# Stick-breaking attention with the scores laid out by key, and running sums made by matrix products

## The chip, the cores and the metric

The kernel runs on one core of one Trainium2 chip. The metric is device time in microseconds (us) of one execution; the times below are medians of repeated runs. The profile is one execution recorded by the hardware profiler.

## The reference

One transformer-like layer on a (2048, 1024) input: a normalised input is projected, three mixers work side by side (attention with 8 heads, a gated convolution, a spatial gate), their results are projected back, and an MLP of width 4096 follows. Only the attention is changed:

```python
z = jnp.einsum('bqhd,bkhd->bhqk', q_blk, k_ctx) * scale
mask = s_pos[None, :] < t_pos[:, None]
log_beta = jax.nn.log_sigmoid(z)
log_stay = jnp.where(mask, jax.nn.log_sigmoid(-z), 0.0)
log_after = lax.cumsum(log_stay, axis=3, reverse=True) - log_stay
w = jnp.where(mask, jnp.exp(log_beta + log_after), 0.0)
outs.append(jnp.einsum('bhqk,bkhd->bqhd', w, v_ctx))
```

With softplus(z) = log(1 + e^z), the weight is exp(z minus the sum of softplus over this key and all later allowed keys). So each query needs a running sum over keys, from the last key backwards.

## The kernel before

The sequence is cut into two halves of 1024 tokens and groups of 512 (`gl` = 0, 1). Every product with weights is made in three passes of 32-bit operands split into a high and a low part (`split`: a cast to the high part on ACT, a subtraction for the low part on DVE). A segment (`run(seg, ...)`) walks over blocks of units; a unit is 256 columns of a weight matrix. Segments 0 and 1 make the projections of the two halves; `take_u` and `take_v` are the spatial gate (tiles pu, pvs, then pmix), VUnit makes pv, QK makes pq and pk, Conv makes pc. Segments 2 and 3 make the output projection (tile po). Then `Up` and `Down` make the MLP (pa, pb, pc, py).

Attention runs behind this as generators. A task is one head and 256 queries (two blocks of 128); each block of queries looks at its own 128 keys and the 128 before. There are 64 tasks. `Background.tick()` is called after each product of a unit: it takes every active generator one `yield` further and starts one task from the queue. So the steps of a task stand one tick apart, with one large product (24 matmuls of 128x512, or 48 of 128x256) between ticks:

- at its first tick: scores z (queries on partitions, two sets of 256 keys as columns) with a mask added by a bf16 product, then `weights`: softplus on ACT and DVE (L434 to L437), a backward scan for each block of queries (L440), the total of each query saved in `carry` (L441), z minus the scan (L442), exp (L443);
- two ticks later: four transposes of the weights into the PSUM tile wt (L467) and their split into wT;
- one tick later: the product with the values (av, L479), and its two halves added (L483, L484).

`all_gone(half)` takes the minimum of `carry` over all tasks of a half. A far-key branch (`far_keys`) is taken only if that minimum is too small, which does not happen in the runs. On PE the minimum needs one transpose (tile pcm), which stands between the first block's group 0 and group 1 of segments 1 and 2. The order of instructions on each engine is fixed when the program is built, by a scheduler that follows the order of the code where it can. Each engine runs its list in order. DMAs are issued from SP (`load`) and from POOL (`store`).

## Time and profile before

| | |
|---|---|
| median of 3 runs | 2228.54 us (2227.8 to 2235.25) |
| the profiled execution | 2228.7 us, its span 2226.9 us |
| mean granted TensorE clock | 0.984 |
| busy: PE, DVE, ACT, POOL | 95%, 65%, 46%, 16% of the span |
| attention's first and last product on PE | at 142.9 and 757.6 us |

The span is the time from the first to the last instruction of the profiled execution; 1.8 us of its time lie outside. PE is the tensor engine, DVE the vector engine, ACT the scalar engine. A busy time is the union of the instructions' times. Matmuls overlap, so what one of them costs PE is the distance between starts in a timeline, and not its duration.

### The profile page before, as it was taken

The numbers are of one execution on the slowest core, as the hardware profiler recorded it, in microseconds if no ns is written. First come the engines' busy times: TensorE is split into PE (matmuls) and PEld (weight loads), VectorE is DVE, ScalarE is ACT, GpSimd is POOL, SyncE is SP. The second block draws the span as 40 slices with busy tenths as digits, with TensorE's granted clock in tenths as the row PEclk, the third lists the DMA queues.
The fourth block names the chain that finished last, engine by engine and source line by source line (L and its number), as shares of the span: only waits on it lengthen the run. The fifth ranks groups of instructions, "written<-read, shape, count | busy, mean of one in ns | idle before, by whom it ended". The sixth has DMA issues, their size and how long they took to land.

```text
span 2226.9 us, 30078 instructions
## 1 busy us (share of the span) xinstructions
PE 2119.3 (95%) x11039; PEld 1802.1 (81%) x11039; DVE 1456.2 (65%) x2417; ACT 1020.5 (46%) x1728; POOL 348.0 (16%) x589
## 2 busy tenths in 40 slices
PE   3999999999999989988999999999999999999998
PEld 3887888788788989876788878888788888888886
DVE  6788877677767643676767787677743434347675
ACT  4645656746556324265444454444523323224432
POOL 2020211021211112223322222222200000000010
PEclk9999999999999999999999999999999999999999
DMA  7473553343434466978956586565764435447572
GB/s 274 130 211 119 148 161 109 98 131 90 126 110 142 155 212 215 357 268 281 332 186 214 201 297 213 189 218 193 259 204 152 152 121 171 142 123 230 195 246 85
DMA packets 223215, 415.35 MB, mean 187 GB/s; under 512 B 18400, under 2 KB 106416, under 8 KB 223056
## 3 DMA queue, kind: packets, MB, share of 16 engines
q1 hardware_dynamic: 177424, 264.28, 37.1%
q0 software_dynamic: 45504, 149.00, 19.1%
q8 instruction: 89, 1.46, 0.3%
q14 instruction: 70, 0.57, 0.1%
q10 hardware_dynamic: 128, 0.04, 0.0%
HBM read 262.18 MB, written 142.67 MB: 182 GB/s over the span
## 4 chain that ended last, share of the span: by engine, by line
PE 51%; issue 11%; DMA 4%; DVE 3%; POOL 2%; ACT 1%; POOLq 0%; SPq 0%; DVEq 0%; ACTq 0%
PE py L1190 27%; PE pb L1082 9%; PE pc L1082 6%; PE pa L1082 5%; PE pc L269 1%; DMA hr<-hs 1%; POOL x L771 1%; DMA f<-in_mlp_w_dram 1%; PE pv L278 1%; PE pq L269 0%; DMA hs<-hs 0%; POOL hd L994 0%; DMA hr<-hd 0%; DVE h L130 0%; POOL hs L1008 0%
## 5 line engine op out<-in xcount | busy, mean ns | idle before, releaser
L1190 PE MATMUL py<-h,w 128*128 128x512 f32 x2688 | 610.7, 389 | 0.0
L1190 PEld LDWEIGHTS py<-h,w 128*128 128x128 f32 x2688 | 504.7, 188 | 105.5 <-issue 1.0
L130 DVE TENSOR_TENSOR w<-ar,w 128x1024 fp32r<-128x1024 f32 x112 | 137.0, 1223 | 264.1 <-ACT w L127 263.8
L127 ACT CAST w<-ar 128x1024 fp32r<-128x1024 f32 x112 | 118.0, 1053 | 368.9 <-PE py L1190 347.8
L127 ACT CAST w<-raw 128x512 fp32r<-128x512 f32 (+1 forms) x215 | 155.2, 736 | 127.9 <-PE pc L1082 46.6
L278 PE MATMUL po<-w,h 128*128 128x256 f32 x1536 | 194.3, 288 | 4.1 <-PEq L681 2.4
L1082 PE MATMUL pb<-h,w 128*128 128x512 f32 x768 | 188.9, 395 | 9.3 <-DVE s L1051 7.8
L130 DVE TENSOR_TENSOR w<-raw,w 128x512 fp32r<-128x512 f32 (+1 forms) x215 | 177.1, 835 | 29.5 <-ACT w L127 28.4
L1082 PE MATMUL pa<-h,w 128*128 128x512 f32 x768 | 189.5, 394 | 6.4 <-ACT s L1049 4.9
L1082 PE MATMUL pc<-hx,w 128*128 128x512 f32 x768 | 190.6, 396 | 4.6 <-DVE hid L1056 4.6
L278 PEld LDWEIGHTS po<-w,h 128*128 128x128 f32 x1536 | 190.2, 196 | 4.7 <-issue 4.2
L1082 PEld LDWEIGHTS pb<-h,w 128*128 128x128 f32 x768 | 145.7, 191 | 42.2 <-DVE s L1051 7.6
L1082 PEld LDWEIGHTS pa<-h,w 128*128 128x128 f32 x768 | 144.8, 189 | 39.2 <-ACT s L1049 5.7
L1082 PEld LDWEIGHTS pc<-hx,w 128*128 128x128 f32 x768 | 143.8, 188 | 39.6 <-DVE hid L1056 5.5
L269 PE MATMUL pc<-h,w 128*128 128x512 f32 x576 | 137.3, 394 | 0.0
L269 PEld LDWEIGHTS pc<-h,w 128*128 128x128 f32 x576 | 106.6, 188 | 21.2
L1057 ACT ACTIVATE hid<-hid 128x512 f32<-128x512 f32 x96 | 60.6, 631 | 106.0 <-DVE hid L1056 106.0
L1082 PE MATMUL pb<-hx,w 128*128 128x512 f32 x384 | 96.9, 402 | 4.5 <-DVE s L1051 4.5
L1289 POOL DMA_DIRECT2D out_dram<-y x24 | 13.0, 540 | 559.9 <-DVE y L1288 558.6
L278 PE MATMUL pv<-w,h 128*128 128x256 f32 x768 | 99.5, 285 | 0.0
L278 PEld LDWEIGHTS pv<-w,h 128*128 128x128 f32 x768 | 94.5, 191 | 0.1
L269 PE MATMUL pk<-h,w 128*128 128x512 f32 x384 | 94.4, 399 | 0.1
(217 smaller groups left out, 3319.7 us busy)
## 6 DMA issues: line engine op xcount, KB each, us to landing
ar<-ad SPq DMA_DIRECT2D x112, 512.0 KB, 4.0
ad<-hid POOLq DMA_DIRECT2D x128, 256.0 KB, 3.2
raw<-in_mlp_w_dram SPq DMA_DIRECT2D x62, 512.0 KB, 5.3
ad<-hsum POOLq DMA_DIRECT2D x96, 256.0 KB, 3.4
aw<-in_ada_w_dram SPq DMA_DIRECT2D x32, 512.0 KB, 4.7
f<-in_mlp_w_dram SPq DMA_DIRECT2D x32, 512.0 KB, 4.9
w2s<-f POOLq DMA_DIRECT2D x64, 256.0 KB, 3.4
w<-w2s SPq DMA_DIRECT2D x32, 512.0 KB, 3.7
```

What stands on the lines that cost most here:

```text
L127: A.copy(hi, src)
L130: V.tensor_tensor(lo, src, hi.bitcast(F32), ALU.subtract)
L269: T.matmul(ps, lhsT=w[k][:, a, c0:c0 + P], rhs=hT[k][:, b], start=n == 0, stop=n == 3 * KT - 1)
L278: T.matmul(ps, lhsT=hT[k][:, a, tb * P:(tb + 1) * P], rhs=w[k][:, b], start=n == 0, stop=n == 3 * KT - 1)
L771: store(out=x1d[g][t0:t0 + 2 * P, cl].rearrange("(b p) n -> p b n", p=P), in_=t.rearrange("p (b n) -> p b n", b=2))
L1057: A.activation(t, t, AF.Relu)
L1082: T.matmul(ps[key], lhsT=w[:, a, k * P:(k + 1) * P], rhs=h[k // 2][:, b, k % 2], start=start and m == 0, stop=m == 11, skip_group_check=no ...
L1190: T.matmul(ps[tb], lhsT=self.a[q][:, a, u * G + tb * P:u * G + (tb + 1) * P], rhs=self.w[at, c][:, b, u], start=c == 0 and u == 0 and n == ...
L1289: (load if end else store)(out=out2[t0:t0 + P, sl], in_=y)
```

## The change

Scores are made with keys on partitions: the keys are the stationary operand and the queries the moving one, so z holds for each block of queries its columns for the 128 keys before (z4[:, b, 0]) and for its own 128 keys (z4[:, b, 1]). The mask is added by one product with F32R operands. Softplus is split into two tiles and multiplied by a triangular matrix of -1 (`neg_after`), which adds the negative running sum within a block of keys onto z in PSUM, and by a matrix of -1 (`neg_ones`), which adds the total of the own block to the block before. The exponential of z is then already laid out for the product with the values, and the transposes are gone. The totals of the queries lie in one row: a copy of row 0 of z from before the sums, minus row 0 after; this row is stored to memory (`cs`) for each task, and `all_gone` loads it back.

z now lives from the first tick to two ticks later, so its pool has three buffers in place of two; the bank of wt is given up. `ones` becomes `neg_ones` (with a subtraction where it was an addition), sums of `mod_sum` are kept in the loaded tile, and some small tiles move to the pool of `etile`.

```diff
-        pz = ph.enter_context(tc.tile_pool(name="pz", bufs=2, space=PSUM, reuse_waits="tile"))
+        pz = ph.enter_context(tc.tile_pool(name="pz", bufs=3, space=PSUM, reuse_waits="tile"))
...
-            A.activation(e, z, AF.Abs)
-            A.activation(e, e, AF.Exp, scale=-1.0)
-            A.activation(e, e, AF.Ln, bias=1.0)
-            V.scalar_tensor_tensor(e, z, 0.0, e, ALU.max, ALU.add)
-            for a, b in lo:
-                r = e[:, a:b][:, ::-1]
-                V.tensor_tensor_scan(r, r, r, init, ALU.add, ALU.bypass)
-            V.tensor_copy(save, e.rearrange("p (b k) -> p b k", b=len(lo))[:, :, 0])
+        def softplus(e, z):
+            A.activation(e, z, AF.Abs)
+            A.activation(e, e, AF.Exp, scale=-1.0)
+            A.activation(e, e, AF.Ln, bias=1.0)
+            V.scalar_tensor_tensor(e, z, 0.0, e, ALU.max, ALU.add)
...
             z = pz.tile([P, G], F32, name="z", tag="z")
-            last = None
-            for b in range(2):
-                o = (2 * qp + b) * P
-                c0 = 256 * b if first and b == 0 else 256 * b + P
-                zb = z[:, b * 256:(b + 1) * 256]
-                with tc.issue_after(last.ins) if last is not None else nullcontext():
-                    T.matmul(zb, lhsT=qq[:, 0, o:o + P], rhs=kk[:, o:o + 256], start=True, stop=False)
-                    T.matmul(zb, lhsT=qq[:, 1, o:o + P], rhs=kk[:, o:o + 256], start=False, stop=False)
-                    last = T.matmul(z[:, c0:(b + 1) * 256], lhsT=identb, rhs=mask[:, c0 - 256 * b:256],
-                                    start=False, stop=True)
+            z4 = z.rearrange("p (b w t) -> p b w t", b=2, w=2)
+            n = 0
+            for kb, c0, w, o in ((1, P, 256, 0), (0, 0, P, 0), (2, 384, P, P)):
+                for s in range(2):
+                    T.matmul(z[:, c0:c0 + w], lhsT=kk[:, q0 + kb * P:q0 + (kb + 1) * P],
+                             rhs=qq[:, s, q0 + o:q0 + o + w], start=n == 0, stop=False)
+                    n += 1
+            T.matmul(z4[:, :, 1], lhsT=identr, rhs=mask.unsqueeze(1).to_broadcast([P, 2, P]),
+                     start=False, stop=True)
             e = etile()
-            weights(e, z, ((0, 256), (256, G)), 0.0, carry[:, half, h, ib:ib + 2])
+            softplus(e, z)
+            sT = halves("sT")
+            split(sT[:, 0], sT[:, 1], e, A)
+            row = etile("row")[0:1]
+            A.copy(row[:, 0:256].rearrange("p (b t) -> p b t", b=2), z4[0:1, :, 0])
             yield
             yield
-            wt = pw.tile([P, G], F32, name="wt", tag="wt")
-            for m in range(4):
-                T.transpose(wt[:, m * P:(m + 1) * P], e[:, m * P:(m + 1) * P], ident)
-            wT = pl.tile([P, 2, G], F32R, name="wT", tag="wT")
-            split(wT[:, 0], wT[:, 1], wt, A)
+            s4 = sT.rearrange("p s (b w t) -> p s b w t", b=2, w=2)
+            for s in range(2):
+                T.matmul(z, lhsT=neg_after, rhs=sT[:, s], start=False, stop=False,
+                         skip_group_check=True)
+            for s in range(2):
+                T.matmul(z4[:, :, 0], lhsT=neg_ones, rhs=s4[:, s, :, 1], start=False, stop=s == 1,
+                         skip_group_check=True)
+            e = etile()
+            A.activation(e, z, AF.Exp)
+            V.tensor_tensor(row[:, 256:].rearrange("p (b t) -> p b t", b=2),
+                            row[:, 0:256].rearrange("p (b t) -> p b t", b=2), z4[0:1, :, 0],
+                            ALU.subtract)
+            store(out=cs[half][h:h + 1, ib * P:(ib + 2) * P], in_=row[:, 256:])
+            wT = halves("wT")
+            split(wT[:, 0], wT[:, 1], e, A)
...
-            store(out=cs[half].rearrange("h p i -> p h i"), in_=carry[:, half])
+            first = (1 - half) * 2 * P
+            n = (HALF - first) // 16
+            ca = etile("ca")[:, :n]
+            load(out=ca, in_=cs[half][:, first:].rearrange("h (a n) -> h a n", n=n))
             cm = sp.tile([P, 1], F32, name="cm", tag="cm")
-            V.tensor_reduce(cm, carry[:, half, :, 2 - 2 * half:], AX.XY, ALU.min)
+            V.tensor_reduce(cm, ca, AX.X, ALU.min)
```

The first place is one tick of segment 0 on PE, after the product pq of group 0 (h_... are the buffers of the input tile). Before:

```order
L269 MATMUL pq<-h_300,w 128x512 x6
L479 MATMUL av<-wT,vt 128x256 x2
L479 MATMUL av<-wT,vt 128x128 x4
L467 MATMUL wt<-ident,e 128x128 x4
L457 MATMUL z<-kk,qq 128x256
L458 MATMUL z<-kk,qq 128x256
L459 LDWEIGHTS identb
L459 MATMUL z<-mask,identb 128x128
L457 MATMUL z<-kk,qq 128x256
L458 MATMUL z<-kk,qq 128x256
L459 LDWEIGHTS identb
L459 MATMUL z<-mask,identb 128x128
```

The same tick in the changed kernel:

```order
L275 MATMUL pq<-h_302,w 128x512 x6
L506 MATMUL av<-wT,vt 128x256 x2
L506 MATMUL av<-wT,vt 128x128 x4
L484 MATMUL z<-sT,neg_after 128x512 x2
L487 MATMUL z<-sT,neg_ones 128x2x128 x2
L469 MATMUL z<-qq,kk 128x256 x2
L469 MATMUL z<-qq,kk 128x128 x4
L472 MATMUL z<-mask,identr 128x2x128
L275 MATMUL pk<-h_299,w 128x512 x6
```

The four transposes of an older task give way to four products of its softplus, and the scores of the new task are six products and one with the mask.

The second place (place A) is on PE in segment 1, from the last product pvs of group 0 to the first product pu of group 1. Before:

```order
L278 MATMUL pvs<-w,h_3627 128x256 x6
L670 MATMUL pcm<-ident,cm 1x128 [waits DVE_49]
L269 MATMUL pu<-h_4014,w 128x512 [waits PE_49,Activation_49]
L269 MATMUL pu<-h_4014,w 128x512 x5
L269 MATMUL pu<-h_4015,w 128x512 x6
L269 MATMUL pu<-h_4016,w 128x512 x6
L652 MATMUL pmix<-swT,vn 128x256 [waits DVE_49]
L652 MATMUL pmix<-swT,vn 128x256 x3
```

In the changed kernel (rows of products pmix left out in the middle):

```order
L284 MATMUL pvs<-w,h_3733 128x256 x5
L679 MATMUL pmix<-swT,vh 128x256 [waits DVE_49]
...
L679 MATMUL pmix<-swT,vh 128x256 [waits PE_49]
L679 MATMUL pmix<-swT,vl 128x256 [waits DVE_49]
...
L679 MATMUL pmix<-swT,vl 128x256
L700 MATMUL pcm<-identr,cm 1x128 [waits DVE_49]
L275 MATMUL pu<-h_4136,w 128x512 [waits Activation_49]
L275 MATMUL pu<-h_4136,w 128x512 x5
```

21 products pmix, 12 of the first pair of token blocks and 9 of the second, now stand ahead of pcm and pu, where 18 products pu stood ahead of the first pmix.

The third place (place B) is on PE in segment 2, around the transposed minimum pcm. Before:

```order
L278 MATMUL po<-w,h_7293 128x256 x6
L479 MATMUL av<-wT,vt 128x256 [waits DVE_49,Activation_49]
L479 MATMUL av<-wT,vt 128x256 [waits DVE_49]
L479 MATMUL av<-wT,vt 128x128 x4
L467 MATMUL wt<-ident,e 128x128 [waits PE_49]
L467 MATMUL wt<-ident,e 128x128 x3
L670 MATMUL pcm<-ident,cm 1x128
L278 MATMUL po<-w,h_7628 128x256 x6
```

In the changed kernel:

```order
L506 MATMUL av<-wT,vt 128x128 x4
L484 MATMUL z<-sT,neg_after 128x512 x2
L487 MATMUL z<-sT,neg_ones 128x2x128 x2
L506 MATMUL av<-wT,vt 128x256 [waits DVE_49,Activation_49]
L506 MATMUL av<-wT,vt 128x256 [waits DVE_49]
L506 MATMUL av<-wT,vt 128x128 x4
L700 MATMUL pcm<-identr,cm 1x128 [waits DVE_49]
L284 MATMUL po<-w,h_7879 128x256 x6
```

The running sums of the last task, its product av and the minimum over all stored rows now follow each other with no product po between them; before, the last av stood 48 products po later and pcm waited for nothing new.

## Rows read from the trace of the kernel before

**Rows 1.** The page: span and busy time of the engines.
```profile
span 2226.9 us, 30078 instructions
PE 2119.3 (95%) x11039; PEld 1802.1 (81%) x11039; DVE 1456.2 (65%) x2417; ACT 1020.5 (46%) x1728; POOL 348.0 (16%) x589
```

**Rows 2.** Windows: busy us of each engine (x count), granted clock, DMA share, GB/s.
```profile
140.00:760.00 620.00, 599.57 (x3648) 525.24 (x3647) 459.85 (x869) 356.18 (x644) 94.28 (x155) 0.98 0.43 131
219.00:225.00 6.00, 6.00 (x25) 5.33 (x25) 4.63 (x10) 3.44 (x7) 1.16 (x2) 0.50 0.13 30
360.00:420.00 60.00, 54.48 (x315) 46.26 (x313) 48.43 (x92) 49.70 (x91) 4.64 (x9) 0.94 0.35 108
```

**Rows 3.** Attention's PE groups: count, busy us, mean ns, idle before, what ended it.
```profile
L479 PE MATMUL av<-wT,vt 128*128 128x128 f32 (+1 forms) x368 | 53.4, 274 | 6.1 <-DVE wT L130 3.1 <-ACT wT L127 2.0 <-DVE a_sb L484 0.9
L457 PE MATMUL z<-kk,qq 128*128 128x256 f32 x128 | 46.6, 365 | 5.4 <-DVE kk L527 3.4 <-DVE carry L441 1.2 <-DVE e L442 0.8
L467 PE MATMUL wt<-ident,e 128*128 128x128 f32 x256 | 41.3, 283 | 4.0 <-DVE wT L130 3.7 <-DVE kk L520 0.3
```

**Rows 4.** PE's timeline around two ticks: start us, duration, line, count.
```profile
304.27 0.79 PE L479 MATMUL av<-wT,vt 128*128 128x256 f32 x6
304.90 0.33 PE L457 MATMUL z<-kk,qq 128*128 128x256 f32 x1
...
305.59 5.73 PE L269 MATMUL pc<-h,w 128*128 128x512 f32 x24
...
318.24 0.60 PE L467 MATMUL wt<-ident,e 128*128 128x128 f32 x4
318.60 0.36 PE L457 MATMUL z<-kk,qq 128*128 128x256 f32 x1
...
319.32 5.72 PE L269 MATMUL pc<-h,w 128*128 128x512 f32 x24
324.88 0.79 PE L479 MATMUL av<-wT,vt 128*128 128x256 f32 x6
```

**Rows 5.** The page: the group of all products po, for the cost of one of 256 columns.
```profile
L278 PE MATMUL po<-w,h 128*128 128x256 f32 x1536 | 194.3, 288 | 4.1 <-PEq L681 2.4 <-DVE mo L768 1.5 <-ACT hf L991 0.2
```

**Rows 6.** Attention's DVE and ACT groups that the change touches.
```profile
L440 DVE TENSOR_TENSOR_SCAN e<-e 128x256 f32<-128x256 f32 x128 | 81.6, 676 | 1.2
L130 DVE TENSOR_TENSOR wT<-wt,wT 128x512 fp32r<-128x512 f32 x64 | 43.9, 686 | 8.4 <-ACT wT L127 7.7
L484 DVE TENSOR_TENSOR a_sb<-av,avlo 64x256 f32<-64x256 f32 x64 | 26.6, 415 | 15.5 <-ACT avlo L483 14.5
L435 ACT ACTIVATE e<-e 128x512 f32<-128x512 f32 x64 | 40.2, 632 | 1.4
L127 ACT CAST wT<-wt 128x512 fp32r<-128x512 f32 x64 | 37.4, 585 | 5.9 <-PE av L479 3.7 <-PE wt L467 0.8
L483 ACT COPY avlo<-av 64x256 f32<-64x256 f32 x64 | 23.6, 369 | 40.7 <-PE av L479 39.5
```

**Rows 7.** Timeline of PE, ACT and DVE at place A.
```profile
422.03 0.60 ACT L285 ACTIVATE gt<-pvs 128x512 f32<-128x512 f32 x1
...
428.80 4.42 PE L269 MATMUL pu<-h,w 128*128 128x512 f32 x18 [0.65 <-ACT hf L242]
...
433.00 0.69 DVE L130 TENSOR_TENSOR vn<-vg,vn 128x512 fp32r<-128x512 f32 x1
433.06 0.69 PE L652 MATMUL pmix<-swT,vn 128*128 128x256 f32 x4
```

**Rows 8.** Timeline of POOL and PE at place B.
```profile
745.03 0.93 POOL L666 DMA_DIRECT2D cs<-carry  x1 [3.69 <-DVE carry L441]
...
751.23 0.27 PE L670 MATMUL pcm<-ident,cm 128*1 128x128 f32 x1
```

**Rows 9.** Small DMAs: count, KB each, median us from issue to landing.
```profile
kk<-ks SPq DMA_DIRECT2D x8, 64.0 KB, 2.6
cs<-carry POOLq DMA_DIRECT2D x2, 32.0 KB, 3.2
```

More of the change, by code (lines that the diff above doesn't have):

```diff
@@ L1 @@
-from contextlib import ExitStack, nullcontext
+from contextlib import ExitStack
 import concourse.bass as bass
@@ L72, in start @@
         while len(self.queue) > left:
-            gen = self.queue.pop(0)
-            if next(gen, self) is not self:
-                self.active.append(gen)
+            self.tick()
     def finish_all(self, gens):
@@ L107, in trunk @@
     bg = Background()
-    ident = const.tile([P, P], F32, name="ident")
-    make_identity(nc, ident)
+    identr = const.tile([P, P], F32R, name="identr")
+    ident = identr.bitcast(F32)
+    neg_ones = const.tile([P, P], F32R, name="neg_ones")
+    negs = neg_ones.bitcast(F32)
     cols = const.tile([P, 32], F32, name="cols")
@@ L296, in trunk @@
     vs = [dram.tile([H, HALF // P, P, P], F32, name=f"vs{hf}") for hf in range(2)]
-    cs = [dram.tile([H, P, HALF // P], F32, name=f"cs{hf}") for hf in range(2)]
+    cs = [dram.tile([H, HALF], F32, name=f"cs{hf}") for hf in range(2)]
     cat_a = [dram.tile([H * HD, HALF], F32, name=f"cat_a{hf}") for hf in range(2)]
@@ L384, in mod_cols, with mod_rows @@
                 yield
-        def mod_rows(dst, part, room=None):
+        def mod_rows(dst, part):
             load(out=dst, in_=ada_b[0:1, part * D:(part + 1) * D].partition_broadcast(P))
             for j in range(2):
-                s = room or ac.tile([P, G], F32, name="msum", tag="msum")
-                yield from mod_sum(s, part * D + j * G)
+                s = yield from mod_sum(part * D + j * G)
                 ps = bank("pm")
-                T.matmul(ps, lhsT=ones, rhs=s, start=True, stop=True)
-                V.tensor_tensor(dst[:, j * G:(j + 1) * G], ps, dst[:, j * G:(j + 1) * G], ALU.add)
+                T.matmul(ps, lhsT=negs, rhs=s, start=True, stop=True)
+                V.tensor_tensor(dst[:, j * G:(j + 1) * G], dst[:, j * G:(j + 1) * G], ps, ALU.subtract)
                 yield
-        identb = ac.tile([P, P], BF16, name="identb")
-        mask = ac.tile([P, 256], BF16, name="mask")
+        mask = ac.tile([P, P], F32R, name="mask")
+        neg_after = ac.tile([P, P], F32R, name="neg_after")
         swT = ac.tile([P, 2, 4 * P], F32R, name="swT")
@@ L481, in attention @@
                     n += 1
-            lo = pl.tile([HD, 256], F32, name="avlo", tag="avlo")
+            lo = etile("avlo")[0:HD, 0:256]
             A.copy(lo, av[HD:P])
@@ L728, in far_block @@
             V.tensor_tensor(old, av[0:HD], old, ALU.add)
-            lo = pl.tile([HD, 256], F32, name="avlo", tag="avlo")[:, :P]
+            lo = etile("avlo")[0:HD, 0:P]
             A.copy(lo, av[HD:P])
```

77 lines of the change are left out of this document (45 added, 32 removed).

## The prediction

> **What bounds the kernel now.** The page comes first: PE is busy for 95% of the span, DVE for 65% and ACT for 46% [rows 1]. That is an average, so the windows come second. Attention's products lie between 140 and 760 us. There PE is busy for 599.57 of 620 us, DVE for 460 and ACT for 356 [rows 2]: PE is the bound of this stretch, and a product added to it lengthens the kernel unless it fills one of PE's gaps. The gaps are small. PE is idle for 620 - 599.57 = 20.4 us, and a mean granted clock of 0.98 costs at most 0.02 x 620 = 12 us more. When the clock falls, it falls to its lower level: it is 0.50, 1.2 GHz, over the 6 us from 219 to 225 [rows 2], which costs 3 us. The groups of attention say whose fault the gaps are: 6.1 + 5.4 + 4.0 = 15.5 us of the 20.4 stand before av, z and wt, and all but the 2.0 put down to ACT were ended by DVE (13.5 us) [rows 3]. So DVE is late at times, though PE is the bound. What the change can win is a part of 20.4 + 12 = 32 us; what it can lose has no such limit.
>
> **The change part by part.** *PE per task.* The timeline is read by distances between starts, since the products overlap. Before: the scores of a task take 304.90 to 305.59 and 318.60 to 319.32, that is 0.69 and 0.72 us (0.71); the four transposes take 318.24 to 318.60, 0.36 us; six products av (two of 256 columns, four of 128) take 304.27 to 304.90, 0.63 us; 24 products of 512 columns take 319.32 to 324.88, 0.23 us each [rows 4]. A product of 256 columns costs 194.3 / 1536 = 0.127 us [rows 5]. After: six score products of the same sizes as those of av, 0.63, and one of 256 columns for the mask, 0.13; then two of 512 columns, 0.46, and two of 256, 0.25. The change adds 0.63 + 0.13 + 0.46 + 0.25 - 0.71 - 0.36 = 0.40 us per task, and 64 tasks make **26 us**. The products with the values stay. No row before shows a product over two separated pieces of 128 columns. Such a one cannot be cheaper than one of 128 columns nor, as I take it, dearer than two, each (0.63 - 0.25) / 4 = 0.10 us; three of them per task then make the term 21 to 30 us, and I keep 26, the price of whole 256 columns.
>
> The Trainium skill, "TensorE: Matmul & The Clock Gate", in its part on the PE-mode transpose, gives some 275 ns for one 128x128 transpose inside a kernel. Our mean duration, 283 ns [rows 3], is the same figure, but it is a latency: four of them start within 0.36 us [rows 4]. By the page's figure the removed transposes would be worth an estimated 70 us in place of 23, and the change would be a gain of some 16 us.
>
> *DVE per task.* Removed are two scans (2 x 0.676), the subtraction from z and a copy of two columns into carry; added are one low part of a split (0.686, over as many columns as the subtraction that goes, so these cancel) and a subtraction in a row of 256 (0.415, the price of 64x256, since what counts is the length) [rows 6]. DVE gets 0.9 us lighter, the copy aside, 60 us in all. DVE isn't the bound, so this is worth only the waits that it ends. I take all 13.5 us of waits before attention's products, and half of the clock's 12 us: **-19 us**. The ends are 0 and -32.
>
> *ACT per task.* Added are one cast (about 0.6, as the wT cast's 0.585) and the copy of a row (0.369, as avlo's) [rows 6]: 1.0 us, 64 us in all. Over the whole stretch ACT goes from 356 to 420 of 620 us, which the products hide. Not everywhere: from 360 to 420 us, where the inputs of segment 1 are normalised, it is busy for 49.7 of 60 us and PE already loses 5.5 [rows 2]. Some six tasks fall into it and bring it to 56 of 60. I take **4 us** there; the ends are 0 and 10. The wait that the change adds to ACT, for the sum of softplus before its cast, is shorter than the wait for the scan that goes away, and what stands behind it, avlo and the next exp, is a tick from its user.
>
> *Stores.* 64 stores of 1 KB join POOL's queue. POOL is busy for 16% [rows 1]; one such store of carry took 0.93 us of POOL [rows 8], 60 us in all and hidden, except at place B. They hold row tiles of the pool of six that the exp also writes to, so a late store would stop ACT; with some 8 us from tick to tick and 3.2 us to land [rows 9] I charge nothing, and keep it as a risk of the upper end.
>
> *Place A.* 18 products pu stood behind the last pvs and covered the gate's chain (gelu, norm, split). That chain took from 422.03 to the first pmix at 433.06, 11.0 us [rows 7]. Now nine products pmix of the second pair of blocks stand ahead of pu, so PE waits for the same chain, begun only when the last pvs ends. PE has 21 products of 0.127 us to do in it, 2.7 us. That leaves at most 8.3 us of idle; I take **7**, since some of the 11.0 went into other tiles' work. The load of ca lies on SP behind the weight loads, but lands within this chain.
>
> *Place B.* Before, the minimum waited only for DVE, and pcm ran at 751.23 between products po [rows 8]. Now pcm needs the last task's row: exp and subtraction (0.6 + 0.4), the store (3.2 from issue to landing, as the store of carry), the load back (2.6, as the small load kk) [rows 9]: 6.8 us after the last running sum, and with the reduction and the gaps between engines some 8. In this time PE has only one set of av, 0.63 us. I take **7 us** of idle; the ends are 4, if both transfers land in half the time, and 10, if SP is held up by a load ahead of it.
>
> *The clock at A and B.* PE stands still for several us at each; if each brings one fall like that at 219 us, at 3 us, that is **6 us**; the ends are 0 and 7.
>
> Other edits (neg_ones for ones, sums kept in the loaded tile, identity through a small tile) exchange one operation for one like it, on engines that wait there; 0, and the loads of weights a slot later at worst, behind which PE still has a unit of 5 us and more.
>
> Sum: 26 - 19 + 4 + 7 + 7 + 6 = 31 us. Against the profiled execution's own time, 2228.7 us, that is 2260 us; the median of the runs is 2228.54, the same within 0.2 us.
>
> **The rivals.** *The transposes cost their durations* (faster): if they do not overlap with what stands behind them, four are worth 4 x 0.283 = 1.13 us per task, and removing them gains 0.77 us per task more than I count, 49 us: 2260 - 49 = 2211 us. It decides from 0.84 us per set on (0.36, and the sum's 31 us over 64 tasks). Against it stands the start of z 0.36 us after that of wt [rows 4]. The union of all transposes' times, 41.3 us [rows 3], is the most that a reading of overlap could give; that moves the sum by 18 us only.
>
> *Places A and B are covered*: the pieces come earlier than the order makes one think (ACT free at A, the store and load short at B), and PE stays dense. Then 20 us fall away: 2240 us. For it: at both places the engines other than PE have little else to do. Against it: the chain of 11.0 us and the landings are measured.
>
> *ACT becomes the bound*: with 1.0 us more per task its casts wT come late for av. A tick has some 5.6 + 0.63 + 0.76 + 0.71 = 7.7 us on PE, and ACT has four activations of 0.63, the casts and the copies, 4.5 us of attention, in it [rows 6], besides the casts of weights and of q and k. If ACT is late by 0.4 us in every one of the 64 ticks, 26 us come on top: 2285 us. For it: 2.0 us of waits for the wT cast are there already [rows 3]. Against it: mean load of 68% after the change.
>
> **How the numbers follow.** Forecast 0.60, covered places 0.20, ACT the bound 0.13, transposes by duration 0.07. A change of 0.5%, 11 us, is about what a measurement of this kernel can tell from none: 2217 to 2240 us. Faster is the transposes' rival, 0.07. Same is the larger part of the covered places and the low tail of the forecast (more waits ended than I took), 0.20. Slower is the rest, 0.73. The range reaches from 2230 (covered places, and 10 us more of the 32 regained) to 2285 (ACT the bound, or all upper ends of A, B and the products); what lies outside are the transposes' rival and the tails, 2 in 10.
>
> **What would show it.** Right: the groups of the products with neg_after and neg_ones and of the scores, in which the distances in the timeline add up to 0.76 and 0.71 us; PE busy for some 26 us more up to its last av; a gap of 5 to 8 us before pmix or pcm at A and before pcm at B, each followed by a stretch of granted clock 0.50; fewer waits for DVE before attention's products. Wrong: no gap at A and B; a busy sum of PE that grows by less than 15 us; waits for wT casts above 15 us in all; or DVE still ending most of PE's waits in ticks without a normalisation.

## The result

The changed kernel takes 2293.55 us (median of 4 runs, 2287.28 to 2301.45) against 2228.17 us of the kernel before: a ratio of 1.028, with a 95% interval of 1.0262 to 1.0298. It is 65 us slower, where 31 us were forecast; the sign was right, the size was not. Medians of the kernel before lie between 2228 and 2232 us in the sessions below, its single runs between 2223 and 2237, so a difference of 3 us or less between two medians carries no weight; where an interval is given, it decides.

The head of the page after answers to [rows 1]:

```profile
span 2290.8 us, 30401 instructions
PE 2154.3 (94%) x11103; PEld 1835.6 (80%) x11103; DVE 1401.8 (61%) x2291; ACT 1080.0 (47%) x1856; POOL 379.2 (17%) x652
```

DVE is 54 us lighter, ACT 60 us and PE 35 us heavier. The span is 64 us longer, so PE's busy time, in which products at the lower clock count as busy too, explains about half. The PE groups of attention after, which answer to [rows 3] (the removed transposes stood there as wt):

```profile
L506 PE MATMUL av<-wT,vt 128*128 128x128 f32 (+1 forms) x368 | 53.7, 275 | 7.6 <-ACT wT L127 5.4 <-DVE a_sb L511 1.4 <-DVE wT L130 0.7
L469 PE MATMUL z<-qq,kk 128*128 128x128 f32 (+1 forms) x384 | 53.0, 272 | 0.0
L484 PE MATMUL z<-sT,neg_after 128*128 128x512 f32 x128 | 44.7, 424 | 8.4 <-ACT row L479 4.7 <-DVE sT L130 3.7
L487 PE MATMUL z<-sT,neg_ones 128*128 128x256 f32 x128 | 25.8, 283 | 0.0
L679 PE MATMUL pmix<-swT,vh 128*128 128x256 f32 x64 | 15.1, 350 | 20.6 <-DVE vh L129 19.7 <-DVE mx L685 0.7
```

The waits before attention's products did not go; they changed their name (16 us now, 15.5 before), and ACT ends more of them, 10.1 us against 2.0. The largest group of waits is new: 20.6 us in all before pmix.

Where the time went is best seen if both executions are cut at the same products. The cuts are the products that start at 143.6, 425.0, 441.6, 722.4 and 763.5 us in the execution before (attention up to place A, place A, the second half of attention, place B). Windows of the kernel before: length, then busy us of PE, PEld, DVE, ACT and POOL with counts, then the granted clock.

```profile
143.60:425.00 281.40, 269.33 (x1574) 232.29 (x1572) 215.98 (x396) 174.41 (x310) 39.36 (x65) 0.98 0.44 133
425.00:441.60 16.60, 15.96 (x87) 13.14 (x86) 10.60 (x31) 8.53 (x18) 0.55 (x1) 1.00 0.49 144
441.60:722.40 280.80, 273.08 (x1644) 238.89 (x1642) 202.12 (x387) 157.08 (x287) 46.66 (x77) 0.99 0.40 120
722.40:763.50 41.10, 41.10 (x349) 40.90 (x349) 27.92 (x51) 16.45 (x30) 6.18 (x9) 1.00 0.55 180
sum 619.90, PE 599.47 PEld 525.22 DVE 456.62 ACT 356.48 POOL 92.76; mean PE 149.87 PEld 131.31 DVE 114.16 ACT 89.12 POOL 23.19
```

The same products in the changed kernel:

```profile
148.30:444.60 296.30, 280.64 (x1597) 245.29 (x1597) 184.63 (x325) 200.11 (x368) 54.01 (x95) 0.96 0.43 127
444.60:482.40 37.80, 22.05 (x103) 18.74 (x102) 18.73 (x50) 15.12 (x34) 1.06 (x2) 0.73 0.22 64
482.40:766.20 283.80, 278.95 (x1665) 246.68 (x1665) 172.80 (x317) 180.89 (x334) 60.30 (x104) 1.00 0.41 120
766.20:815.90 49.70, 45.63 (x350) 44.72 (x350) 24.17 (x45) 19.33 (x37) 7.96 (x13) 0.93 0.44 141
sum 667.60, PE 627.27 PEld 555.42 DVE 400.33 ACT 415.45 POOL 123.33; mean PE 156.82 PEld 138.86 DVE 100.08 ACT 103.86 POOL 30.83
```

Of the 64 us, 21.2 are lost at place A alone (16.6 us became 37.8), 14.9 in the first half of attention, 3.0 in the second half, 8.6 at place B, 4.7 before the first cut and the rest, 11 us, behind the last. The window of place A holds 16 products more than before (103 against 87), pmix and av that stood outside it; at the 0.127 us of [rows 5] they are some 2 of its 21.2 us. PE's idle time is length less busy: 20.4 us before, 40.3 us after.

### The profile page after: what moved, and what is told of

It is laid out like the page before. It is cut to its first block, busy times and chain, and to the rows that moved or that the text cites. A ratio compares the mean times of both kernels' runs of the same rounds, so it can differ in the third digit from the quotient of the medians.

```text
span 2290.8 us, 30401 instructions
## 1 busy us (share of the span) xinstructions
PE 2154.3 (94%) x11103; PEld 1835.6 (80%) x11103; DVE 1401.8 (61%) x2291; ACT 1080.0 (47%) x1856; POOL 379.2 (17%) x652
## 4 chain that ended last, share of the span: by engine, by line
PE 56%; issue 10%; DMA 5%; DVE 3%; POOL 2%; ACT 1%; SPq 0%; POOLq 0%; DVEq 0%; ACTq 0%
PE py L1220 26%; PE pb L1112 9%; PE pc L1112 6%; PE pa L1112 6%; PE pc L275 2%; PE pq L275 2%; PE pk L275 2%; PE pv L284 2%; DMA hr<-hs 1%; DMA x<-x 1%; DMA f<-in_mlp_w_dram 1%; PE z L469 1%; POOL x L801 1%; PE av L506 1%; PE z L484 0%
## 5 line engine op out<-in xcount | busy, mean ns | idle before, releaser
L275 PE MATMUL pq<-h,w 128*128 128x512 f32 x384 | 93.7, 394 | 0.0
```

The costliest lines, as they stand in the source:

```text
L275: T.matmul(ps, lhsT=w[k][:, a, c0:c0 + P], rhs=hT[k][:, b], start=n == 0, stop=n == 3 * KT - 1)
```

## The experiments

Of the kernels below, those whose names begin with b_ are the kernel before with one edit, the others the changed kernel with edits. Where a difference of two ratios is turned into time, 1% is 22.3 us.

**Place A.** PE, ACT, SP and DVE of the changed kernel there:

```profile
454.40 1.01 PE L679 MATMUL pmix<-swT,vh 128*128 128x256 f32 x3 [5.40 <-DVE vh L129]
...
467.76 0.98 PE L679 MATMUL pmix<-swT,vh 128*128 128x256 f32 x3 [9.28 <-DVE vh L129]
...
469.84 0.41 PE L700 MATMUL pcm<-identr,cm 128*1 128x128 f32 x1
...
445.61 0.59 ACT L291 ACTIVATE gt<-pvs 128x512 f32<-128x512 f32 x1
...
458.31 0.60 ACT L291 ACTIVATE gt<-pvs 128x512 f32<-128x512 f32 x1 [3.37 <-PE pmix L679]
...
463.86 0.74 SPq L696 DMA_DIRECT2D ca<-cs  x1
...
468.26 0.20 DVE L698 TENSOR_REDUCE cm<-ca 128x1 f32<-128x48 f32 x1
```

The last product pvs ends near 449 us. The gate's chain runs twice, once for each pair of token blocks, and the second begins only at 458.31, when the first pair's pmix are done: gt needs one of the six etiles, and vh and vl now hold two. The tile ca of the minimum is an etile as well, and its load waited for one, as the waits of SP show (us in all, times, longest):

```profile
SPq L696 <- DVE vg L297: 12.2, 1, 12.2
```

L297 of the second chain is the last to read gt, and the load of ca starts at 463.86, when L297 is done. PE waits for both chains, then runs pcm, and only then pu. Two theories: (1) the etiles make two chains out of two overlapping ones; (2) the place of pcm ahead of pu costs, since PE runs its list in order.

*vq* takes vh and vl out of the etiles:

```diff
-                    hi, lo = etile("vh", F32R), etile("vl", F32R)
+                    vn = pl.tile([P, 2, G], F32R, name="vn", tag="qq", bufs=3)
+                    hi, lo = vn[:, 0], vn[:, 1]
```

> The changed kernel with the gate's two split tiles vh and vl taken out of the pool of six etiles again, into one tile of the three buffers of qq. PE's order keeps pcm ahead of pu. Theory 1 (at place A the second gate chain must wait for an etile that the first pair's products pmix free, so the two chains run one after the other): the second wait of 9.3 us before pmix and part of the slow-clock stretch behind it go, 8 to 14 us less than the changed kernel: 2280 to 2286 us. Theory 2 (only the place of pcm ahead of pu costs): within 3 us of 2293.5.

Measured: 2288.68 us, 1.0273 (1.0239 to 1.0308). Place A gave back next to nothing. pmix of the second pair now stands behind pu, but pcm does not:

```profile
450.49 3.51 PE L680 MATMUL pmix<-swT,vn 128*128 128x256 f32 x12 [7.19 <-DVE vn L129]
462.80 0.37 PE L701 MATMUL pcm<-identr,cm 128*1 128x128 f32 x1 [8.80 <-DVE cm L699]
```

The reduction to cm needs only the small load ca. That load still waited 9.4 us for DVE and started at 455.10; from there to the reduction at 462.55 it is DVE's list that holds cm, behind the second chain. The second chain itself is hardly earlier: its gt starts 11.1 us after the first one's (12.7 in the changed kernel, 9.6 before) and waits 2.2 us for DVE's a_sb, which frees avlo, another tile that moved to the etiles. So taking vh and vl out is not enough, and vq does not test an emptier pool of etiles. What its trace did win are 4.8 us at the gate of segment 0: at the product that started at 81.9 us before, the changed kernel is 5.1 us late and vq 0.3, and at the first cut 4.7 and 0.4. The medians do not tell the two kernels apart.

*late* calls all_gone one group later:

```diff
                     if seg in (1, 2) and bn == 0 and gl == 0:
                         bg.start(0)
+                    if seg in (1, 2) and bn == 0 and gl == 1:
                         flags[seg - 1] = all_gone(seg - 1)
```

> The changed kernel with the call of all_gone one group later (after group 1 of the first block), so that pu and po stand ahead of pcm; vh and vl stay etiles. Theory 2 (the stalls at A and B come from the place of pcm, which waits for the stored row to come back, and before which the scheduler put all products pmix): place A gives back some 20 us and place B some 8 us: 2263 to 2272 us. Theory 1 alone (the etiles hold the second chain up wherever pcm stands): only place B and the first wait of A, 10 to 14 us: 2280 to 2284 us.

Measured: 2294.37 us, 1.0289 (1.026 to 1.0318): nothing. The products pu covered the first group's chains as theory 2 said, and the stall came back whole at the second group's, where pcm now stood:

```profile
483.82 0.98 PE L679 MATMUL pmix<-swT,vh 128*128 128x256 f32 x3 [7.58 <-DVE vh L129]
496.03 0.98 PE L679 MATMUL pmix<-swT,vh 128*128 128x256 f32 x3 [9.24 <-DVE vh L129]
```

*mid* calls it between the two, inside the loop over the block's units, behind take_u of group 1 (in segment 2, behind the first set of po there):

```diff
+                        if seg in (1, 2) and bn == 0 and gl == 1 and unit is blk[0][0]:
+                            flags[seg - 1] = all_gone(seg - 1)
...
-                        flags[seg - 1] = all_gone(seg - 1)
```

> The changed kernel with the call of all_gone after the first unit of group 1 (take_u in segment 1, the first set of po in segment 2), so that 48 products pu and two sets of po stand on PE between the gate's pieces or the last task and pcm. Theory 2b (the stalls at A and B are the wait of pcm, behind which all of PE's next unit queues; where pcm was put right behind the other group's gate pieces it only took the same stall along): place A gives back 18 to 22 us, place B 6 to 9 us: 2263 to 2270 us. Theory 1 (etiles hold the second gate chain up anyway): at most the first wait and place B, 10 to 14 us, 2280 us or more.

Measured: 2291.97 us, 1.0276 (1.0236 to 1.0316): not told apart from the changed kernel, so theory 2b missed, and the 10 to 14 us that theory 1 allowed were not given back either. The scheduler drew pmix of the second pair and pcm together again, and pmix waited for the chain that the etiles hold back; at place B pcm waited another 3.4 us, its reduction being behind the split of a weight tile on DVE.

```profile
473.37 0.98 PE L679 MATMUL pmix<-swT,vh 128*128 128x256 f32 x3 [5.28 <-DVE vh L129]
...
463.67 0.60 ACT L291 ACTIVATE gt<-pvs 128x512 f32<-128x512 f32 x1 [4.21 <-PE pmix L679]
```

*midrollvq* adds vq's edit and *roll*'s (below):

> The changed kernel with three edits: all_gone called after the first unit of group 1, the sum of mod_sum handed on to the newest loaded tile, and vh and vl in one tile of qq's buffers. If the three stalls are separate they add up: some 20 + 8 from the first, 3 to 5 from each of the others: 2255 to 2265 us. If they are one and the same slack, no more than the first edit alone: 2263 to 2270 us.

Measured: 2284.62 us, 1.024 (1.0208 to 1.0272); neither expectation was met, since pcm still waits.

*nopcm* takes pcm off PE:

```diff
+            V.tensor_reduce(mins[:, half, 4 * h + ib // 2:4 * h + ib // 2 + 1], row[:, 256:], AX.X, ALU.min)
             store(out=cs[half][h:h + 1, ib * P:(ib + 2) * P], in_=row[:, 256:])
...
-            load(out=ca, in_=cs[half][:, first:].rearrange("h (a n) -> h a n", n=n))
...
-            T.transpose(pc, cm, ident)
...
+            mh = mins[:, half].rearrange("p (h i) -> p h i", h=H)
+            V.tensor_reduce(c1, mh[:, :, 1 - half:], AX.XY, ALU.min)
```

> The changed kernel with the minimum taken per task: DVE reduces each row of totals to one number in SBUF, and all_gone reduces 32 such numbers; no load back and no product pcm on PE. Theory 2c (the stalls at A and B come from PE waiting in its fixed order for pcm; the two kernels with pcm moved still waited for it, since the reduction ahead of it stood behind other work on DVE): place A gives back 18 to 22 us and place B 6 to 9 us, with 0 to 2 us lost to 64 short reductions on DVE: 2262 to 2271 us. Theory 1 (the gate's second chain waits for etiles wherever pcm is): A gives back 10 us at most, 2274 to 2282 us.

Measured: 2266.66 us, 1.0153 (1.0133 to 1.0174): (1.028 - 1.0153) x 2229 = 28 us given back, as theory 2c said. Its windows, cut at the same products:

```profile
150.60:443.90 293.30, 280.04 (x1598) 245.37 (x1597) 194.28 (x356) 200.27 (x368) 54.00 (x95) 0.97 0.43 129
443.90:462.90 19.00, 16.73 (x92) 14.09 (x91) 14.24 (x38) 10.96 (x24) 1.06 (x2) 1.00 0.42 124
462.90:748.00 285.10, 279.90 (x1674) 247.51 (x1673) 185.51 (x355) 184.22 (x345) 60.33 (x104) 1.00 0.41 120
748.00:790.20 42.20, 42.20 (x349) 41.84 (x349) 25.37 (x49) 19.49 (x37) 7.96 (x13) 1.00 0.50 167
sum 639.60, PE 618.86 PEld 548.81 DVE 419.41 ACT 414.94 POOL 123.35; mean PE 154.72 PEld 137.20 DVE 104.85 ACT 103.73 POOL 30.84
```

Place A costs 2.4 us more than before in place of 21.2, place B 1.1 in place of 8.6. The second chain is as late as ever, but pu stands ahead of its pmix and PE does not wait for it:

```profile
458.65 0.60 ACT L291 ACTIVATE gt<-pvs 128x512 f32<-128x512 f32 x1 [4.18 <-PE pmix L681]
```

The place by itself costs nothing either. In *a_nocum* (below), whose minimum is a constant, pcm stands where it stood, pu follows it and pmix stands behind; place A costs 2.5 us more than before, as in nopcm:

```profile
433.20 0.27 PE L694 MATMUL pcm<-identr,cm 128*1 128x128 f32 x1 [1.62 <-DVE vg L297]
433.84 3.69 PE L275 MATMUL pu<-h,w 128*128 128x512 f32 x15 [0.37 <-DVE c L696]
```

So it was the wait of pcm: one product that needs a far result, in the list ahead of 48 others that need nothing. How much of that wait the etiles make, through the load of ca and the second chain, and how much DVE's list, is not shown: no kernel gave ca a tile outside the etiles.

**The terms of the sum, one by one.** *b_notr* and *b_noscan*: the kernel before without the transposes, and without the scans.

```diff
-                T.transpose(wt[:, m * P:(m + 1) * P], e[:, m * P:(m + 1) * P], ident)
...
-            split(wT[:, 0], wT[:, 1], wt, A)
+            split(wT[:, 0], wT[:, 1], e, A)
```
```diff
-                V.tensor_tensor_scan(r, r, r, init, ALU.add, ALU.bypass)
...
-            V.tensor_reduce(cm, carry[:, half, :, 2 - 2 * half:], AX.XY, ALU.min)
+            V.memset(cm, 200.0)
```

> The kernel before without the four transposes per task: the split to wT reads the weights e directly, so keys and queries are exchanged in the product with the values (that part of the computation is changed). Theory of the forecast (four transposes cost PE 0.36 us per task, as the distance of starts says): 0.36 x 64 = 23 us less at most, 2205 to 2212 us. Rival (they cost their durations, 1.13 us per task): 72 us less, some 2156 us. If PE's gaps swallow them (other engines set the end): 0 to 10 us less.

Measured: 2209.3 us, 0.991 (0.988 to 0.9939): 20 us less.

> The kernel before without the two scans per task (so the weights lack the running sums; the minimum is a constant). It shows what the relief of DVE is worth by itself, 1.35 us per task. The forecast took 19 us, with ends at 0 and 32: 2209 us for 19, and 2196 to 2229 us for the ends. If the relief is worth much less (PE's gaps have other causes): 2222 us or more.

Measured: 2204.56 us, 0.9883 (0.9863 to 0.9902): 26 us less. The sums over the same four windows, first of b_notr, then of b_noscan:

```profile
sum 600.10, PE 573.07 PEld 500.23 DVE 454.77 ACT 356.44 POOL 92.63; mean PE 143.27 PEld 125.06 DVE 113.69 ACT 89.11 POOL 23.16
```

```profile
sum 595.40, PE 587.89 PEld 518.50 DVE 381.76 ACT 360.14 POOL 92.83; mean PE 146.97 PEld 129.62 DVE 95.44 ACT 90.03 POOL 23.21
```

Without the transposes PE is busy 26.4 us less and idle 6.6 us more. Without the scans PE's idle time falls from 20.4 to 595.40 - 587.89 = 7.5 us: 12.9 us of waits ended. PE is also busy 11.6 us less for as many products, and most of that is the clock: it reads 1.00 in all four windows of b_noscan, against 0.98, 1.00, 0.99 and 1.00 before, which is some (0.02 + 0.01) x 281 = 8 us.

*a_nocum*: the changed kernel without the four products.

```diff
-                T.matmul(z, lhsT=neg_after, rhs=sT[:, s], start=False, stop=False,
...
-                T.matmul(z4[:, :, 0], lhsT=neg_ones, rhs=s4[:, s, :, 1], start=False, stop=s == 1,
...
-            V.tensor_reduce(cm, ca, AX.X, ALU.min)
+            V.memset(cm, 200.0)
```

> The changed kernel without its four products with neg_after and neg_ones per task (so the weights lack the running sums; the exponential gets a factor of 0.001 to stay finite, and the minimum is replaced by a constant, with its store and load kept). Theory of the forecast (PE bound, 0.71 us per task by the predicted prices, 0.75 by the trace after): 45 to 48 us less than the changed kernel, 2245 to 2249 us, and a few us more where z frees earlier. Rival (the products partly fill gaps of PE that other engines make): 20 to 30 us less, 2264 to 2274 us.

Measured: 2229.8 us, 1.0001 (0.9982 to 1.0019). It had to be compared with nopcm, which I had not foreseen: with a constant minimum pcm does not wait for a far result either. Against nopcm it is (1.0153 - 1.0001) x 2229 = 34 us, between the two expectations of 45 to 48 and 20 to 30, so neither was met: a part of what the products take on PE comes back as waits when they are gone (607.10 - 579.48 = 27.6 us of idle in attention, against 20.7 in nopcm).

*b_cast*: the kernel before with wT's cast on ACT done twice.

```diff
+            A.copy(wT[:, 0], wt)
             split(wT[:, 0], wT[:, 1], wt, A)
```

> The kernel before with the high part of wT cast twice on ACT (the second cast writes the same values), 0.585 us of ACT per task more and nothing else; wT's low part comes that much later. Theory 7 (ACT is near its limit where inputs are normalised, so the change's added 1.0 us of ACT per task costs 5 to 15 us): 4 to 10 us more than before, 2233 to 2239 us. Rival (hidden behind PE): within 3 us of 2229.

Measured: 2237.78 us, 1.0038 (1.0027 to 1.0049): 8.5 us for 0.585 us of ACT per task, though ACT was busy for 46% of the span. The second cast also stands ahead of wT's low part, on the way to av: PE's waits before av for ACT's wT grew from 2.0 to 7.4 us. So the run shows the price of a cast in this place, and not of ACT's load alone. *sdve* moves the cast of sT in the changed kernel from ACT to DVE:

```diff
-            split(sT[:, 0], sT[:, 1], e, A)
+            split(sT[:, 0], sT[:, 1], e)
```

> The changed kernel with the high part of softplus (sT) cast on DVE in place of ACT, 0.6 us per task from ACT to DVE. Theory 4 (ACT is late in the stretch from 360 to 420 us, where the trace after shows PE waiting 3.7 us for the row's copy and 2 us for h): 3 to 8 us less, 2286 to 2290 us. Rival (DVE was no less late there, and both wait for each other): within 3 us of 2293.5, or up to 10 us more.

Measured: 2292.48 us, 1.027 (1.0244 to 1.0297): no difference that can be told. In the stretch where inputs are normalised it gains 4 us (late by 4.4 us more from 352.8 to 425 us of the time before, where the changed kernel is late by 8.4), and loses it elsewhere.

**The sums kept in the loaded tile.** Forecast at nothing. The changed kernel at 234 us, DVE and PE:

```profile
234.09 0.49 DVE L370 TENSOR_SCALAR aw<-aw,cact 128x512 f32<-128x512 f32 x1 [3.77 <-DMA aw<-in_ada_w_dram]
...
237.16 0.50 PE L484 MATMUL z<-sT,neg_after 128*128 128x512 f32 x1 [3.67 <-DVE sT L130]
```

DVE waits for a load of ada_w, the low part of sT is queued behind, and PE waits for it. *b_ms*: the kernel before with this edit alone (in mod_sum `s = a[:, 0]` for the first tile, as in the changed kernel).

> The kernel before with one part of the change alone: the sums of mod_sum are kept in the first loaded tile. Theory 3 (this edit, forecast at nothing, costs by itself): 4 to 10 us more than before, 2232 to 2238 us. Rival (it costs only because attention's new work makes DVE and the loads late): within 3 us of 2228.2.

Measured: 2234.68 us, 1.002 (1.0005 to 1.0036): 4.5 us (1 to 8 by the interval). *roll* hands the sum on to the newest tile, so that no landing buffer is held for four steps:

```diff
...
-                        V.scalar_tensor_tensor(s, a[:, b], cact[:, k + b:k + b + 1], s,
+                        V.scalar_tensor_tensor(a[:, b], a[:, b], cact[:, k + b:k + b + 1], s,
                                                ALU.mult, ALU.add)
+                    s = a[:, b]
```

> The changed kernel with the sum of mod_sum handed on to the newest loaded tile (each step writes into the tile just loaded), so that the first landing buffer is free after one step and not after four. Theory 3 (the landing buffer held for four steps delays later loads, and DVE's wait for aw at 234 us and near 1670 us comes from it): 5 to 10 us less than the changed kernel, 2283 to 2289 us. Rival (the load of aw is late because loads of weights stand ahead of it on SP, whatever buffer is held): within 3 us of 2293.5.

Measured: 2288.42 us, 1.0268 (1.0238 to 1.0298): not told apart from the changed kernel, and DVE still waits 4.8 us for aw. One landing buffer is then still occupied between two steps; that this is why DVE waits, and not the place of the load on SP, is not shown by roll. Room for a tile of its own is there where softplus has no low part, or where another tile is given up (*exact*, below). *nosplit* makes that room (on top of nopcm, with wT in a single buffer); *nosplit_ms* uses it:

```diff
-            sT = halves("sT")
-            split(sT[:, 0], sT[:, 1], e, A)
+            sT = pl.tile([P, 1, G], F32R, name="sT", tag="sT", bufs=2)
+            softplus(e, z, sT[:, 0])
...
```

> nopcm with softplus written at once as the high part sT, and the same high part multiplied twice in place of high and low (so the running sums are wrong, and the low part is left out); PE's products are as many as before. It takes the cast of 0.6 us off ACT and the low part of 0.69 us off DVE in each task. Theory 6 (the split of softplus makes ACT and DVE late, and eats what the removed scans gave): 8 to 18 us less than nopcm, 2248 to 2258 us. Rival (PE's products alone decide): within 4 us of 2266.

> nosplit with the sums of mod_sum in a tile of their own again, for which the room of sT's low part is used. Theory 3 (sums kept in the loaded tile cost 4 us or more, as in the kernel before with this edit alone): 4 to 10 us less than nosplit. Rival: within 3 us of it.

Measured: nosplit 2261.36 us, 1.0142 (1.0119 to 1.0164), which is nopcm's 1.0153 within the error; nosplit_ms 2248.98 us, 1.0084 (1.0067 to 1.0101). The tile of its own is worth (1.0142 - 1.0084) x 2229 = 13 us by the medians; the two traces, cut at the same products, differ by 8.3 us. DVE's wait is there in the one and gone in the other (nosplit, then nosplit_ms):

```profile
233.40 0.49 DVE L370 TENSOR_SCALAR aw<-aw,cact 128x512 f32<-128x512 f32 x1 [4.28 <-DMA aw<-in_ada_w_dram]
```

```profile
225.47 0.47 DVE L368 TENSOR_SCALAR msum<-aw,cact 128x512 f32<-128x512 f32 x1
```

**Totals, and all repairs together.** *norow* leaves the totals out altogether (of nopcm, the row's lines go, and the minimum is a constant):

```diff
-            A.copy(row[:, 0:256].rearrange("p (b t) -> p b t", b=2), z4[0:1, :, 0])
...
-            store(out=cs[half][h:h + 1, ib * P:(ib + 2) * P], in_=row[:, 256:])
```

> The kernel with the minimum taken per task (nopcm), and then without the totals altogether: no copy of the row on ACT (0.37 us per task), no subtraction and reduction on DVE (0.4 and 0.2), no row tile held among the six etiles, no store; the minimum is a constant, so that part of the computation is left out. Theory 5 (of the 35 us that nopcm is slower than the kernel before, a good part is the totals' work and the row tile that holds an etile for two ticks): 8 to 15 us less than nopcm, 2251 to 2259 us. Rival (they are hidden beside PE): within 4 us of 2266.

Measured: 2261.26 us, 1.0145 (1.0123 to 1.0168): not told apart from nopcm. The row's work is hidden as far as the two intervals tell, to within some 7 us. *best* is nopcm with vq's and roll's edits:

> The same with two edits more: vh and vl in one tile of qq's buffers, and the sum of mod_sum handed on to the newest loaded tile. If the etiles hold up what the missing pcm leaves, 5 to 10 us less than without the two edits: 2254 to 2263 us. If not, the same as without them, 2262 to 2271 us. In both cases slower than the kernel before, since the products' 20 us or more stay.

Measured: 2263.34 us, 1.0143 (1.0119 to 1.0167): not told apart from nopcm, though its trace shows the 5 us of the first gate gained. *exact* adds the tile for the sums to nopcm and vq, and gives up a_sb for it:

```diff
-            V.tensor_tensor(a_sb[j * HD:(j + 1) * HD, qp * 256:(qp + 1) * 256], av[0:HD], lo, ALU.add)
+            V.tensor_tensor(lo, av[0:HD], lo, ALU.add)
+            store(out=cat_a[half][h * HD:(h + 1) * HD, ib * P:(ib + 2) * P], in_=lo)
```

> The changed kernel with all four prices paid back and nothing of the computation left out: the minimum per task without pcm, vh and vl in one tile of qq's buffers, the sums of mod_sum in a tile of their own, for which the tile a_sb is given up (each task adds its two halves in avlo and stores 64 KB by itself). If the parts add up: 2263 us of the kernel with pcm and the etiles mended, less 8 to 12 us for the sums, 2251 to 2255 us, slower than before by about what the products cost. If the 48 stores more on POOL, which hold etiles, cost in turn: 2258 to 2268 us.

Measured: 2265.53 us (5 runs, 2255.96 to 2266.75), 1.0156 (1.0138 to 1.0175). Its profiled execution is the 2255.96 us one, near the sum of the parts; the other runs are not. So the sums' price does not show in this kernel, and whether the stores by task took it back is open. *single* is nosplit_ms with vq's edit and half of the running sums' products:

```diff
-            for s in range(2):
-                T.matmul(z, lhsT=neg_after, rhs=sT[:, s], start=False, stop=False,
+            T.matmul(z, lhsT=neg_after, rhs=sT[:, 0], start=False, stop=False, skip_group_check=True)
...
```

> The changed kernel with pcm, the sums and vh and vl mended, and softplus kept as its high part alone: one product with neg_after and one with neg_ones per task (the low part of softplus is left out of the running sums). If PE's products decide what is left: 0.35 us per task less, 64 x 0.35 = 22 us less than the sum of the mended parts (2251 to 2255 us): 2229 to 2236 us, level with the kernel before. If the remaining 20 us come from elsewhere: 2240 us or more.

Measured: 2226.82 us (12 runs), 0.9984 (0.9971 to 0.9997): level with the kernel before, 0.16% under it, at the price of softplus's low part. It is the only version with running sums that does not lose.

## Why the prediction was right in sign and wrong in size

| | forecast, us | measured, us |
|---|---|---|
| place A, with its clock | 7 + 3 | 21.2 (15.1 more idle, some 4 of clock, some 2 of moved products) |
| place B, with its clock | 7 + 3 | 8.6 (4.1 idle, some 3.5 of clock) |
| PE's products, less DVE's relief, plus ACT | 26 - 19 + 4 = 11 | 14.9 + 3.0 = 17.9 |
| ahead of attention | 0 | 4.7 |
| behind place B | 0 | 11 |

*Place A failed.* The step was: "PE waits for the same chain, begun only when the last pvs ends", of which at most 8.3 us are left, while "the load of ca [...] lands within this chain". I counted one chain, since I saw pmix as what PE waits for. It was pcm, at the end of everything that DVE and ACT had to do: two chains, the second of them late by the etiles, 5.4 + 0.7 + 9.3 = 15.4 us of idle where 7 were forecast. The load of ca did not stand ready behind the weight loads; it waited 12.2 us for an etile that the second chain held. That the small tiles' move to the six etiles would couple ACT, SP and PE was in the diff; only the row tiles' share had been named, at nothing, and the gate's tiles and ca stand in no term. In the kernel before pcm stood in PE's list too [rows 8] and cost nothing, because it waited for nothing; here all 48 products pu stood behind it:

```profile
469.91 12.72 PE L275 MATMUL pu<-h,w 128*128 128x512 f32 x48
```

The Trainium skill, "PSUM — Partial Sum Buffer", part on engine and sequencer instructions, states such an order: matmuls start in program order, and the queues of the scalar, vector and GpSimd engines are strict. Here the trace agrees, with pu's 12.72 us of products behind one product of 0.41 us.

*The clock at A and B came out a little over its upper end of 7 us.* One dip of 3 us was forecast at each. After PE stopped at A, the windows of the changed kernel show:

```profile
450.00:453.00 3.00, 0.00 (x0) 0.00 (x0) 1.39 (x6) 2.13 (x8) 0.00 (x0) 0.95 0.93 254
453.00:456.00 3.00, 1.59 (x7) 1.59 (x8) 2.92 (x6) 1.91 (x4) 0.00 (x0) 0.50 0.30 84
456.00:459.00 3.00, 1.76 (x7) 1.20 (x6) 2.83 (x10) 0.60 (x1) 0.58 (x1) 0.50 0.23 87
...
465.00:468.00 3.00, 0.24 (x1) 0.27 (x2) 2.31 (x8) 0.41 (x2) 0.00 (x0) 0.50 0.04 8
468.00:471.00 3.00, 3.00 (x13) 2.72 (x14) 1.02 (x5) 0.00 (x0) 0.00 (x0) 0.50 0.00 0
471.00:474.00 3.00, 3.00 (x10) 2.38 (x9) 0.00 (x0) 0.00 (x0) 0.00 (x0) 0.63 0.00 0
```

The granted clock is at its lower level, 0.50 (1.2 GHz), in every slice from 453 to 471 us, which is most of the stall and the first products behind it. As an estimate, that cost half of PE's busy time in the slices at 0.50 and 0.37 of that in the slice at 0.63: 0.5 x (1.59 + 1.76 + 0.24 + 3.00) + 0.37 x 3.00 = 4.4 us. At B the mean of 0.93 over 49.7 us makes some 3.5. So what was undersized at A is the idle time, not the clock.

*Place B was right in sum, and split otherwise.* Forecast were 7 us of idle (ends 4 and 10) and 3 of clock.

```profile
797.80 0.38 PE L506 MATMUL av<-wT,vt 128*128 128x256 f32 x1 [1.34 <-ACT wT L127]
...
797.83 0.52 POOL L494 DMA_DIRECT2D cs<-row  x1 [0.26 <-DVE row L491]
...
799.75 0.34 SPq L696 DMA_DIRECT2D ca<-cs  x1
...
801.42 0.22 DVE L698 TENSOR_REDUCE cm<-ca 128x1 f32<-128x64 f32 x1 [2.95 <-DMA ca<-cs]
...
801.70 0.37 PE L700 MATMUL pcm<-identr,cm 128*1 128x128 f32 x1 [2.39 <-DVE cm L698]
```

This store of 1 KB had landed when the load was issued, 1.9 us after it, and the load of 32 KB took 1.7 us to its reduction; [rows 9] gave 3.2 for a store of 32 KB and 2.6 for a load of 64 KB. The idle time was 49.70 - 45.63 = 4.1 us in all, the lower end. It was luck that the store was quick: the 64 stores of rows took this long to land (shortest, median, longest):

```profile
DMA to landing us min/median/max: 1.5/3.1/9.1
```

With some 3.5 us of clock and the 1.1 us by which nopcm too is slower here, that is all of the 8.6 us. One edit that stands in no term is `Background.start`: it now steps the running tasks as well, where it only started the waiting ones. It may be why the last av stands ahead of pcm at B; no run tests it by itself.

*PE's products were right in kind; that they fit the sum is luck.* A task's running sums take 0.75 us from start to start (788.41 to 789.16 us), its scores 0.81 (369.37 to 370.18 us in nopcm); 0.71 and 0.76 were forecast. By these distances the term would be (0.75 + 0.81 - 0.71 - 0.36) x 64 = 31 us in place of 26. With pcm away, PE is busy for 618.86 - 599.47 = 19.4 us more in attention. The 6 us that the clock should give back do not explain the gap to 26: the clock reads 0.97, 1.00, 1.00 and 1.00 in nopcm's windows and 0.98, 1.00, 0.99 and 1.00 before, so nothing came back. By busy time the term was some 7 us too large and the clock's share of the relief some 6 too large, and the two cancel. Why busy time grew by less than the distances add up to is not shown. The upper end of the term was also summed wrongly: three products at 0.20 us in place of 0.127 make 14 us more, some 39 and not 30. The rival that transposes cost their durations is refuted: 20 us, not 72, which goes with 0.36 us per set. The figure of the Trainium skill, "TensorE: Matmul & The Clock Gate", in its part on the PE-mode transpose, given there for bf16 and taken per transpose, would have made it an estimated 70; the run does not bear that out.

*DVE's relief was real and did not arrive.* In the kernel before, the scans' end alone ends 12.9 us of waits and gives back some 8 of clock (b_noscan); I had taken 13.5 and 6. But with pcm away PE's idle time in attention is 639.60 - 618.86 = 20.7 us, as much as before. The new work made new waits: in nopcm PE waits 4.7 us for ACT's row, 3.9 for DVE's a_sb behind avlo, 3.2 for the input's x and 2.4 for ACT's wT. ACT's 4 us was probably too little, since 0.585 us of ACT per task, put ahead of wT, cost 8.5 us by itself. The parts don't add up, though: taking the split's 0.6 us off ACT again (nosplit) or the row's work (norow) gives nothing that can be told. What is shown is that both sides are equal in sum, not which of the new waits took which part.

*"Other edits: 0" failed.* The sums in the loaded tile cost 4.5 us in the kernel before, 8 to 13 us beside the new attention without a low part; vh and vl in the etiles cost 5 us at the first gate by the traces, which the medians of vq and best do not tell from none. Of the 11 us behind place B, some 3 are the sums again, in the last phase (late by 4.6 us more between the first and the 96th product py, 1.6 in nosplit_ms); in the trace of b_ms the same edit alone makes 5 us behind place B. The other 6 to 8 us come in small steps; their cause stays open.

## What to carry to other kernels

A product that waits for a far result should stand where no ready work stands behind it in PE's list, or not be on PE at all: here two kernels that moved it only moved the stall, and the one that did without it won 28 us. When tiles move to another pool to make room, ask for each who then waits for a free buffer, and what that engine's next instruction feeds; here the buffers that the running sums needed drove other tiles out of their own; the accumulator in the loaded tile cost 4.5 us or more, and the gate's tiles and ca in the etiles made the far result later. The relief of an engine that is not the bound is worth only the waits that remain ended once the change's own new work is on the engines.

## What was not expected of the hardware

A store of 1 KB is not reliably quicker to land than one of 32 KB: 3.1 us in the median of 64, from 1.5 to 9.1, against 3.2. And ACT, busy for less than half of the time, has little slack ahead of av in this kernel: 37 us of added casts over 64 tasks lengthened it by 8.5 us. Without the scans the clock stayed at 1.00 through all four windows of attention, and that gave some 8 us on top of the 12.9 of waits that ended.
